# One hybrid layer on Trainium2: the turn at LN1 with four plain FF tiles, a scan with fewer vector steps, and early forms for the output projection

## The chip, the cores and the metric

One core of a Trainium2 chip runs the kernel. The time is device time in microseconds (us) of one execution; lower is better. Five engines run their own queues in order: TensorE (PE, matrix products; weight loads are shown as PEld), VectorE (DVE), ScalarE (ACT), GpSimd (POOL) and SyncE (SP), which issues most DMA transfers. [...]

## The reference

One layer with a sequence of 1024 positions, width 1024 and FF width 4096, all in float32:

```python
mods = (silu(c) @ ada_w + ada_b); sh1, sc1, g1, sh2, sc2, g2 = split(mods, 6)
h = x * (1 + sc1) + sh1
# Mamba-2 mixer: z, xBC, dt = h @ w_in; causal conv of 4 and silu on xBC;
# chunked state-space scan, 8 groups of 4 heads of 64, state 128; y += D * xs;
# y = rmsnorm_per_group(y * silu(z)) * norm_w;  y = y @ w_out
x = layer_norm(alpha * x + g1 * y, ln1_g, ln1_b)
h = x * (1 + sc2) + sh2
x = layer_norm(alpha * x + g2 * (square(relu(h @ w1)) @ w2), ln2_g, ln2_b)
```

## The kernel before

Every large product is made of three products of 128 x 128 by 128 x 512: each operand is split into a high part (fp32r, made by an ACT or DVE cast, L117) and a low part (the rest, one subtraction on DVE or POOL, L120), and high x high, low x high and high x low are added in PSUM. "Forms" below means such a pair. The order of instructions on each engine is set by a planner that takes, engine by engine, the earliest instruction in program order that it believes ready; `issue_after` adds that an instruction stands behind a named one on its engine. Tiles live in pools; a pool opened after another is closed takes over its memory, and each of its tiles waits for the last readers of what lay there.

The stages:

- Head and scan (up to some 739 us). 45 weight tiles of the input projection (`proj`, L137) are streamed; between them the planner places 64 steps of the chunked scan (`ssd_chunk`, L318: 8 groups x 8 chunks), 16 gates (`gate`, L382: 8 groups x 2 halves of the sequence) and 8 conditioning blocks (`mods_block`, L419), one after every fifth weight tile. A chunk transposes x and B into the PSUM bank px, makes X (times dt), cbm, bt and xd (X times wend) on DVE, and the state product pst (L372) needs bt and xd. A gate squares and sums into the bank pr, takes the reciprocal root by Ln, Exp and a Newton step, scales y and stores it to DRAM on SP's queue (L416). A block loads four times 512 KB into one buffer, multiplies and adds on DVE (L427, L429) and sums over partitions with PE into the bank pr. Blocks 0 to 3 give shift and scale of the second half (mod2), 4 to 7 the gates g1b and g2b.
- Output projection (739 to some 950 us). Four passes, (T, Dh) = (0,0), (0,1), (1,0), (1,1), over halves of the sequence (T) and of the columns (Dh), `out_pass` L545; each has 16 steps of 12 matmuls. A step loads a piece of w_out and, in the passes with Dh = 0, of y (`out_load`, L522), and splits both: w_out's high part on ACT and low part (owl) on POOL. The forms of y for T = 0 lie in the blocks B of the pool `per`, which takes the place of the projection's input forms hh and hl. The passes use the PSUM pairs psm (T, 0) and ps2 (T, 1).
- LN1 and the turn (around 950 to 1030 us). `ln1(T)` (L583) normalises four rows, transposes them (L601) and makes h2 and its forms in B. Two FF tiles (`up_plain`, f = 0, 1) run T = 0 in PE's spare time and T = 1 after `ln1(1)`, then two more (f = 2, 3) run both halves. Meanwhile DVE makes sums of the four blocks of h2 (L707 to L712), whose forms t1 to t4 the rest of the FF tiles need: from f = 4 on tiles go in pairs (`up_quad`, L732) with seven block products in place of eight, and each pair needs sums of its w1 blocks (L738 to L741) and forms s1 to s4, a1 and a22.
- Down projection (some 1290 us to the end), `down`, then LN2.

Names: `NS = 4` (L668) is the number of plain tiles; `mpa` holds the w1 forms of f = 0, 1 in rings of two; `hk` and `lt` hold h2 of T = 0 and T = 1; `tpool` the forms t; `wp` the raw and split weights of the input projection; `load1` and `forms1` (L643, L648) load and split a w1 tile; `lg`, `lbb` (L638) are LN1's rows for the residual.

Of the kernel before, what the change touches and what calls it, by code (L numbers as in the profile page):

```python
# [34 lines left out]
def trunk(ctx: ExitStack, tc: tile.TileContext, a: dict, out: bass.AP):  # L35
# [23 lines left out]
    adab = consta([P, 6, KT], "adab")  # L59
# [5 lines left out]
    vec.memset(ones, 1.0)  # L65
    ones_r = consta([P, P], "ones_r", F32R)
# [13 lines left out]
    csil = consta([P, KT], "csil")  # L80
# [38 lines left out]
    def low(src, hi, lo, eng):  # L119
        eng.tensor_tensor(lo, src, hi.bitcast(F32), op=ALU.subtract)  # L120
# [197 lines left out]
    def ssd_chunk(g, c):  # L318
# [21 lines left out]
        if not last:  # L340
# [3 lines left out]
            vec.tensor_tensor(xd, X, wend[:, c, hs].unsqueeze(2).broadcast_to([P, HPG, HD]), op=ALU.mult)  # L344
# [37 lines left out]
    def gate(g, T):  # L382
# [25 lines left out]
        vec.tensor_tensor(q, m, q, op=ALU.mult)  # L408
        vec.scalar_tensor_tensor(r, q, 3.0, r, op0=ALU.subtract, op1=ALU.mult)
        for j in range(2):  # L410
# [4 lines left out]
            else:  # L415
                sp.dma_start(y_dram[2 * g + j][:, ts], gt[:, j, :])  # L416


    def mods_block(b):  # L419
# [23 lines left out]
    vec.tensor_scalar(nwcol, nwcol, -0.5, None, op0=ALU.mult)  # L443
# [21 lines left out]
    for n, (kind, g, j) in enumerate(slots):  # L465
# [56 lines left out]
    def out_load(T, Dh, k):  # L522
# [5 lines left out]
        if Dh == 0 and not (T == 0 and k >= 14):  # L528
# [173 lines left out]
    for T in range(2):  # L702
        up_plain((2, 3), ws2, T)
# [243 lines left out]
```

## Time and profile before

| | us |
|---|---|
| median of 3 runs (1655.02 to 1657.81) | 1656.39 |
| the profiled execution, its own time | 1657.81 |
| its span | 1656.1 |
| PE busy | 1574.5 (95%) |
| DVE busy | 1017.6 (61%) |
| ACT busy | 758.5 (46%) |
| POOL busy | 564.3 (34%) |

The profiled execution is one of the three runs. Times in the trace count from the start of its span. Busy time is the union of an engine's instructions; a wait is the idle time of an engine in front of an instruction, with the instruction that ended it. Most of the matmuls overlap, so a single one lasts 0.39 to 0.40 us but they start 0.23 us apart.

### The profile page before, as it was taken

How to read it: one execution, taken by the hardware profiler on the slowest of the kernel's cores; microseconds unless marked ns; L12 is line 12 of the kernel's file. 1: busy time of each engine (PE TensorE's matmuls, PEld its weight loads, DVE VectorE, ACT ScalarE, POOL GpSimd, SP SyncE). 2: the span in 40 equal slices, each digit the busy share in tenths (PEclk: the TensorE clock that was granted, in tenths of full speed). 3: DMA queues.
4: the chain of work that ended last, by engine and by line, in shares of the span. 5: the costliest groups of instructions: out<-in, count | busy, mean ns of one | idle time of the engine just before them, and what ended most of it. 6: DMA issues, size and time to landing. Idle time of an engine off the chain costs nothing.

```text
span 1656.1 us, 20252 instructions
## 1 busy us (share of the span) xinstructions
PE 1574.5 (95%) x7600; PEld 1264.8 (76%) x7600; DVE 1017.6 (61%) x1480; ACT 758.5 (46%) x1159; POOL 564.3 (34%) x305
## 2 busy tenths in 40 slices
PE   7999898999999899988899978999999999999997
PEld 5887686878777787766688856888888888878886
DVE  8757969787776757757754384545554542287335
ACT  3546557675647466765443153333333322333230
POOL 3313424342424224244645352322332222244221
PEclk9999999999999999999999989999999999999998
DMA  8324423333233222115764122232223655446541
GB/s 323 129 80 147 133 84 115 103 97 107 92 113 96 83 77 77 45 58 178 243 207 160 57 95 83 90 114 102 102 102 132 217 192 166 146 140 207 183 131 51
DMA packets 77138, 209.37 MB, mean 126 GB/s; under 512 B 9585, under 2 KB 11121, under 8 KB 76145
## 3 DMA queue, kind: packets, MB, share of 16 engines
q1 hardware_dynamic: 76176, 205.96, 37.2%
q0 software_dynamic: 576, 2.10, 0.3%
q8 instruction: 60, 0.98, 0.2%
q14 instruction: 38, 0.30, 0.1%
q10 hardware_dynamic: 288, 0.03, 0.0%
HBM read 174.89 MB, written 33.16 MB: 126 GB/s over the span
## 4 chain that ended last, share of the span: by engine, by line
PE 69%; DVE 17%; DMA 6%; issue 4%; ACT 3%; POOL 1%; SPq 0%; DVEq 0%; POOLq 0%; ACTq 0%
PE mm L836 20%; PE mm L144 19%; PE mm L729 16%; PE mm L542 7%; DMA adr<-in_ada_r_dram 2%; DVE mac L429 2%; PE mm L684 2%; DVE macc L203 1%; PE pst L372 1%; DVE y L411 1%; DVE hn L378 1%; DVE dec L349 1%; PE py L359 1%; DMA yr<-y_dram 1%; DMA ada<-in_ada_a_dram 1%
## 5 line engine op out<-in xcount | busy, mean ns | idle before, releaser
L144 PE MATMUL mm<-hh,whi 128*128 128x512 f32 x720 | 288.5, 401 | 0.0
L144 PE MATMUL mm<-hl,whi 128*128 128x512 f32 x720 | 287.4, 399 | 0.0
L144 PE MATMUL mm<-hh,wlo 128*128 128x512 f32 x720 | 286.3, 398 | 0.0
L836 PE MATMUL mm<-w2h,uh 128*128 128x512 f32 x512 | 197.9, 389 | 1.2 <-DVE tm L866 1.2
L836 PE MATMUL mm<-w2l,uh 128*128 128x512 f32 x512 | 198.2, 389 | 0.0
L836 PE MATMUL mm<-w2h,ul 128*128 128x512 f32 x512 | 197.6, 389 | 0.0
L120 POOL TENSOR_TENSOR wlo<-wraw,whi 128x1024 fp32r<-128x1024 f32 x45 | 111.8, 2484 | 233.1 <-ACT whi L117 233.1
L144 PEld LDWEIGHTS mm<-hh,wlo 128*128 128x128 f32 x720 | 136.5, 190 | 29.2 <-issue 1.8
L144 PEld LDWEIGHTS mm<-hh,whi 128*128 128x128 f32 x720 | 136.5, 190 | 28.9 <-issue 1.6
L144 PEld LDWEIGHTS mm<-hl,whi 128*128 128x128 f32 x720 | 136.5, 190 | 28.7 <-issue 1.1
L353 POOL TENSOR_TENSOR ea<-ea,Ct 128x512 f32<-128x512 f32 x56 | 79.4, 1418 | 192.3 <-ACT ea L352 187.0
L120 POOL TENSOR_TENSOR w2l<-w2r,w2h 128x1024 fp32r<-128x1024 f32 x30 | 75.0, 2502 | 185.8 <-ACT w2h L117 185.8
L120 DVE TENSOR_TENSOR ul<-ur,uh 128x512 fp32r<-128x512 f32 x62 | 49.8, 812 | 129.1 <-ACT uh L117 129.1
L347 ACT ACTIVATE dec<-ar,acs 128x128 f32<-128x128 f32 x256 | 81.6, 390 | 82.3 <-PE py L359 79.0
L120 POOL TENSOR_TENSOR owl<-owr,owh 128x512 fp32r<-128x512 f32 x64 | 90.1, 1416 | 85.0 <-ACT owh L117 82.7
L836 PEld LDWEIGHTS mm<-w2h,uh 128*128 128x128 f32 x512 | 96.1, 188 | 21.7 <-DVE tm L866 1.6
L836 PEld LDWEIGHTS mm<-w2l,uh 128*128 128x128 f32 x512 | 96.2, 188 | 20.2
L836 PEld LDWEIGHTS mm<-w2h,ul 128*128 128x128 f32 x512 | 96.1, 188 | 19.7
L117 ACT CAST uh<-ur 128x512 fp32r<-128x512 f32 x62 | 38.4, 621 | 154.0 <-PE mm L836 123.1
L117 ACT CAST w2h<-w2r 128x1024 fp32r<-128x1024 f32 x62 | 64.8, 1048 | 22.4 <-DMA w2r<-in_w_dram 13.4
L429 DVE SCALAR_TENSOR_TENSOR mac<-adr,csil,mac 128x512 f32<-128x512 f32 x56 | 60.2, 1076 | 21.8 <-DMA adr<-in_ada_r_dram 21.4
L349 DVE TENSOR_TENSOR dec<-dec,cbm 128x512 f32<-128x512 f32 x64 | 61.0, 953 | 19.3 <-ACT dec L348 19.3
(356 smaller groups left out, 3487.7 us busy)
## 6 DMA issues: line engine op xcount, KB each, us to landing
w2r<-in_w_dram SPq DMA_DIRECT2D x62, 512.0 KB, 3.7
wraw<-in_w_in_dram SPq DMA_DIRECT2D x45, 512.0 KB, 4.2
w1r<-in_w_dram SPq DMA_DIRECT2D x34, 512.0 KB, 3.7
adr<-in_ada_r_dram SPq DMA_DIRECT2D x32, 512.0 KB, 3.6
ar<-a_dram SPq DMA_DIRECT2D x64, 256.0 KB, 3.3
owr<-in_w_out_dram SPq DMA_DIRECT2D x64, 256.0 KB, 3.3
ur<-u_dram SPq DMA_DIRECT2D x62, 256.0 KB, 2.8
u_dram<-row SPq DMA_DIRECT2D x28, 512.0 KB, 3.8
```

What stands on the lines that cost most here:

```text
L117: return (act.copy if eng is act else eng.tensor_copy)(hi, src)
L120: eng.tensor_tensor(lo, src, hi.bitcast(F32), op=ALU.subtract)
L144: pe.matmul(ps[:, hf, :], lhsT=w_[:, k, :], rhs=x_[:, k, ts], start=(k == 0 and i == 0), stop=(k == KT - 1 and i == 2))
L203: vec.scalar_tensor_tensor(av_, ada[:, k, :], csil[:, k:k + 1], av_, op0=ALU.mult, op1=ALU.add)
L347: act.activation(dec[:, h, :], ar[:, h, :], AF.Relu, scale=-1.0, bias=acs[:, c, g * HPG + h:g * HPG + h + 1])
L349: vec.tensor_tensor(dec, dec, cbm.unsqueeze(1).broadcast_to([P, HPG, C]), op=ALU.mult)
L353: pool.tensor_tensor(ea, ea, G["C"][:, ts].unsqueeze(1).broadcast_to([P, HPG, C]), op=ALU.mult)
L429: vec.scalar_tensor_tensor(acc, ad[:, i, :], csil[:, k:k + 1], acc, op0=ALU.mult, op1=ALU.add)
L542: pe.matmul(po[t // 2][:, t % 2, :], lhsT=l_[:, t * P:t * P + P], rhs=r_, start=(k == 0 and i == 0), stop=(k == 15 and i == 2))
L684: pe.matmul(ups[f][:, T, :], lhsT=w_[:, k, :], rhs=x_[:, k % 4, :], start=(k == 0 and i == 0), stop=(k == KT - 1 and i == 2))
L729: pe.matmul(dst, lhsT=w_[:, k, :], rhs=x_[:, k, :], start=(first and k == 0 and i == 0), stop=(k == 3 and i == 2), skip_group_check=not first)
L836: pe.matmul(po[t][:, Dh, :], lhsT=l_[:, t * P:(t + 1) * P], rhs=r_[:, Dh * 512:Dh * 512 + 512], start=(f == 0 and i == 0), stop=(f == NF - ...
```

## The change

- Scan: six conditioning blocks, in the order 4, 5, 6, 7, 0, 1, one after every seventh weight tile; blocks 2 and 3 are made by a new function `mods_ln1` behind the second output pass, with their loads in the eight tiles of `hk` and their sum in a psm tile. wend is multiplied by dt once, and xd is made from px and that in place of X. In the gate Ln reads pr with scale and bias; m is gone, and the Newton step reads pr. The y of groups 6 and 7 is stored from POOL's queue.
- Output projection: steps 0 and 1 of the first pass load into `wraw`, and their forms are made in the buffers `whi`, `wlo` and in a tile of group 6's x, ahead of the projection's end. The second pass loads and splits y for these two steps again.
- Turn: the w1 loads stand behind w_out's. All four plain tiles run T = 0 together, behind step 13 of the fourth pass, and then T = 1 in pairs; tiles 2 and 3 have forms of their own (`pf`). The sums of h2 are held behind the last low part of h2; low parts for T = 1 go to DVE. The first pair's sums lie in tiles with the tags of lg and lbb, its forms in those of h2 (`lt`, `hk`), its a1 low part on DVE. t1 takes the place of `pf`. The second pair takes its second product ahead of s3's. lg and lbb are loaded and scaled in the down projection.

```diff
-            vec.tensor_tensor(xd, X, wend[:, c, hs]..., op=ALU.mult)
+            vec.tensor_tensor(xd, px[:, 0:2 * P]..., wend[:, c, hs]..., op=ALU.mult)
...
-        m = ssp.tile([P, 512], F32, name="m", tag="s1")
-        vec.tensor_scalar(m, pr, 1.0 / 256.0, EPS, op0=ALU.mult, op1=ALU.add)
-        act.activation(r, m, AF.Ln)
+        act.activation(r, pr, AF.Ln, scale=1.0 / 256.0, bias=eps_c)
...
-        vec.tensor_tensor(q, m, q, op=ALU.mult)
-        vec.scalar_tensor_tensor(r, q, 3.0, r, op0=ALU.subtract, op1=ALU.mult)
+        vec.scalar_tensor_tensor(q, pr, 256.0 * EPS, q, op0=ALU.add, op1=ALU.mult)
+        vec.scalar_tensor_tensor(r, q, 768.0, r, op0=ALU.subtract, op1=ALU.mult)
...
-                sp.dma_start(y_dram[2 * g + j][:, ts], gt[:, j, :])
+                (pool if g >= NG - 2 else sp).dma_start(y_dram[2 * g + j][:, ts], gt[:, j, :])
...
-        if n % 5 == 0 and n // 5 < 8:
-            mods_block(n // 5)
+        if n % 7 == 0 and n // 7 < 6:
+            mods_block((4, 5, 6, 7, 0, 1)[n // 7])
...
+    yx = gp.tile([P, 2, S], F32R, name="yx", tag="xs")
+    early = []
+    for k in range(2):
+        raw = wp.tile([P, 2, 512], F32, name="wraw", tag="wraw", bufs=4)
+        sp.dma_start(raw[:, 0, :], a["w_out"][k][:, 0:512])
+        sp.dma_start(raw[:, 1, :], y_dram[k][:, 0:512])
+        w = [wp.tile([P, 512], F32R, name="w" + q, tag="w" + q) for q in ("hi", "lo")]
+        y = (yx[:, k, 0:512], yx[:, k, 512:S])
+        split(raw[:, 0, :], *w, act, pool)
+        split(raw[:, 1, :], *y, act, vec)
+        early.append((w, y))
     phR.close()
...
+        if k == 13:
+            queue["k13"] = mm_.ins
...
+    def mods_ln1(b):
+        ad = []
+        for k in range(KT):
+            t_ = hk.tile([P, 512], F32, name="adm", tag=f"h2{k % 2}{k // 2}")
+            sp.dma_start(t_, a["ada_r"][b, k // 2][:, k % 2, :])
+            if k == 0:
+                vec.tensor_scalar(t_, t_, csil[:, 0:1], None, op0=ALU.mult)
+            else:
+                vec.scalar_tensor_tensor(t_, t_, csil[:, k:k + 1], ad[-1], op0=ALU.mult, op1=ALU.add)
+            ad.append(t_)
+        pm = psm.tile([P, 2, 512], F32, name="mm", tag="mm")
+        for i in range(4):
+            pe.matmul(pm[:, 0, i:i + 1], lhsT=ad[-1][:, i * P:(i + 1) * P], rhs=one1, start=True, stop=True)
+        mod2_add(b, pm[:, 0, 0:4])
...
-                low(h2, bh[:, kk, :], bl[:, kk, :], vec if kh == 0 else pool)
+                queue["h2l"] = low(h2, bh[:, kk, :], bl[:, kk, :], vec if kh == 0 or T == 1 else pool).ins
...
     out_pass(0, 1, po)
+    for b in (2, 3):
+        mods_ln1(b)
...
-        sp.dma_start(w1r, a["w1"][f])
+        load_behind(w1r, a["w1"][f], "w")
...
-    up_plain((0, 1), ws1, 0)
-    ln1(1, sts)
-    up_plain((0, 1), ws1, 1)
-    ws2 = [forms1(load1(f)) for f in range(2, NS)]
-    for T in range(2):
-        up_plain((2, 3), ws2, T)
+    for f in range(2, NS):
+        ws1.append(forms1(load1(f), [pf.tile([P, KT, P], F32R, name=f"p{q}{f}", tag=f"p{q}{f}") for q in "hl"]))
+    with tc.issue_after(queue["k13"]):
+        up_plain(0)
+    ln1(1, sts)
+    up_plain(1)
+    up_evict(0)
...
+    with tc.issue_after(queue["h2l"]):
+        for kk in range(4):
+            b11, b12, b22 = h2f[0, 0, kk], h2f[0, 1, kk], h2f[1, 1, kk]
+            t1_ = vec.tensor_tensor(b11, b12, b11, op=ALU.subtract)
+            vec.tensor_tensor(b12, b22, b12, op=ALU.subtract)
+    t_split("t3", lambda kk: h2f[0, 1, kk], vec)
+    with tc.issue_after(t1_.ins):
+        for kk in range(4):
+            b11, b21, b22 = h2f[0, 0, kk], h2f[1, 0, kk], h2f[1, 1, kk]
+            vec.tensor_tensor(b22, b22, b11, op=ALU.subtract)
+            vec.tensor_tensor(b21, b21, b22, op=ALU.subtract)
+    t_split("t2", lambda kk: h2f[1, 1, kk], vec)
...
+    r0_, a22_ = quad_sums(NS // 2, s_)
+    a1_ = forms1(r0_, eng=vec)
+    quad_splits(s_, F_)
+    up_evict(1)
+    pfx.close()
+    tl = tst.enter_context(tc.tile_pool(name="tl", bufs=1, side="right", reuse_waits="tile"))
+    TF["t1"] = [tl.tile([P, 4, 512], F32R, name="t1" + q, tag="t1" + q) for q in "hl"]
     TF["t4"] = h2_block("b12")
+    t_split("t1", lambda kk: h2f[0, 0, kk], pool)
+    t_split("t4", lambda kk: h2f[1, 0, kk], pool)
...
+            if T == 0 and f == 2:
+                load_behind(lg, a["ln_rows"][0:1, :].partition_broadcast(P).squeeze(1), "w2")
+                load_behind(lbb, a["ln_rows"][1:2, :].partition_broadcast(P).squeeze(1), "w2")
+                vec.tensor_scalar(lg, lg, ALPHA, None, op0=ALU.mult)
+                vec.tensor_scalar(lbb, lbb, ALPHA, None, op0=ALU.mult)
```

## Rows read from the trace of the kernel before

**Rows 1.** Stages: start:end, length, busy us (instructions) by engine, clock, DMA share, GB/s

```profile
115.00:739.00 624.00, 597.98 (x3355) 476.68 (x3354) 453.00 (x775) 387.43 (x615) 210.83 (x109) 0.99 0.30 97
739.00:820.00 81.00, 67.92 (x302) 50.63 (x301) 60.32 (x74) 42.78 (x73) 43.17 (x27) 0.96 0.59 195
820.00:950.00 130.00, 130.00 (x584) 106.61 (x584) 52.96 (x78) 42.68 (x70) 63.03 (x47) 1.00 0.46 148
950.00:1060.00 110.00, 92.26 (x366) 69.86 (x365) 71.04 (x77) 46.31 (x70) 43.15 (x22) 0.91 0.23 79
1060.00:1290.00 230.00, 230.00 (x987) 185.21 (x987) 119.86 (x128) 76.34 (x129) 69.08 (x35) 1.00 0.34 118
1290.00:1656.00 366.00, 354.06 (x1559) 292.27 (x1558) 176.07 (x207) 108.58 (x147) 101.21 (x42) 0.99 0.47 157
```

**Rows 2.** The same view of two short stretches; the order is PE, PEld, DVE, ACT, POOL

```profile
743.00:746.40 3.40, 3.22 (x7) 2.28 (x8) 2.98 (x3) 3.26 (x7) 3.40 (x3) 0.50 0.23 63
...
982.00:992.20 10.20, 7.40 (x16) 5.13 (x17) 9.36 (x5) 6.75 (x8) 8.81 (x4) 0.50 0.45 129
```

**Rows 3.** PE's waits, 950 to 1030: in total us, times, longest us

```profile
PE mm L684 <- ACT w1h L117: 5.1, 2, 4.1
PE mm L684 <- DVE b12l L120: 4.0, 2, 3.2
```

**Rows 4.** PE's time line in the turn: start, us, instruction [idle before]

```profile
956.59 0.65 PE L601 MATMUL mm<-ident,row 128*128 128x128 f32 x4 [1.57 <-ACT row L593]
...
959.79 0.77 PE L684 MATMUL mm<-b12h,w1h 128*128 128x512 f32 x1
```

**Rows 5.** DVE's groups, 957 to 992: count, busy us, mean ns, idle before

```profile
L712 DVE TENSOR_TENSOR h<-h,h 128x512 f32<-128x512 f32 x4 | 6.0, 1492 | 0.0
...
L708 DVE TENSOR_TENSOR h<-h,h 128x512 f32<-128x512 f32 x4 | 2.7, 678 | 0.0
```

**Rows 6.** POOL's groups, 957 to 1031, the same view

```profile
L120 POOL TENSOR_TENSOR t2l<-h,t2h 128x512 fp32r<-128x512 f32 x4 | 6.4, 1599 | 2.0 <-ACT t2h L117 1.9
```

**Rows 7.** PE's waits in the scan, 115 to 739

```profile
PE pst L372 <- DVE xd L344: 9.3, 8, 3.4
...
PE pst L372 <- DVE hn L379: 5.1, 3, 3.5
```

**Rows 8.** DVE's groups in the scan, 115 to 739

```profile
L429 DVE SCALAR_TENSOR_TENSOR mac<-adr,csil,mac 128x512 f32<-128x512 f32 x56 | 60.2, 1076 | 21.8 <-DMA adr<-in_ada_r_dram 21.4
...
L344 DVE TENSOR_TENSOR xd<-X,wend 128x256 f32<-128x256 f32 x56 | 33.6, 599 | 0.0
L336 DVE TENSOR_TENSOR X<-px,dt 128x256 f32<-128x256 f32 x63 | 26.2, 415 | 12.7 <-PE py L359 7.1 <-PE px L334 5.3
...
L402 DVE TENSOR_SCALAR m<-pr 128x512 f32<-128x512 f32 x12 | 8.2, 687 | 29.6 <-PE pr L400 29.6
```

**Rows 9.** Waits of DVE for the loads of the conditioning blocks: us, times

```profile
  DMA adr<-in_ada_r_dram: 29.3, 15
```

**Rows 10.** PE's waits, 739 to 820

```profile
PE mm L542 <- POOL owl L120: 6.0, 6, 2.1
PE mm L542 <- ACT y L117: 3.7, 1, 3.7
```

**Rows 11.** POOL's time line: the second of two w1 low parts there

```profile
795.93 2.84 POOL L120 TENSOR_TENSOR w1l<-w1r,w1h 128x1024 fp32r<-128x1024 f32 x1
```

**Rows 12.** DVE's time line: a conditioning block's first and last instruction, two evictions' starts

```profile
451.61 0.48 DVE L427 TENSOR_SCALAR mac<-adr,csil 128x512 f32<-128x512 f32 x1
...
479.52 0.73 DVE L429 SCALAR_TENSOR_TENSOR mac<-adr,csil,mac 128x512 f32<-128x512 f32 x1
...
805.77 1.28 DVE L621 TENSOR_TENSOR tm<-mm,g1b 128x512 f32<-128x512 f32 x2
...
849.97 1.29 DVE L621 TENSOR_TENSOR tm<-mm,g1b 128x512 f32<-128x512 f32 x2 [2.51 <-PE mm L542]
```

**Rows 13.** DMA issues from POOL's queue: ns min/median/max, first and last start

```profile
L688 POOL DMA_DIRECT2D u_dram<-row x4: 531/596/736, 1281.0 to 1303.8; - x4
```

More of the change, by code (lines that the diff above doesn't have):

```diff
@@ L305, in trunk @@
             act.activation(dst.rearrange("p a b -> p (a b)"), pa, fn)
+    vec.tensor_tensor(wend, wend, dt, op=ALU.mult)
     acsf = acs.rearrange("p a b -> p (a b)")
@@ L527, in out_load @@
         yr = None
-        if Dh == 0 and not (T == 0 and k >= 14):
+        if (Dh == 0 and not (T == 0 and k >= 14)) or (T == 0 and k < 2):
             yr = ob_pool.tile([P, 512], F32, name="yr", tag="yr")
@@ L547, in out_pass @@
         for k in range(16):
-            ws.append(out_load(T, Dh, k))
+            first = T == 0 and Dh == 0 and k < 2
+            ws.append(early[k][0] if first else out_load(T, Dh, k))
             ks = [k] if k < 16 - KL else range(16 - KL, 16) if k == 15 else []
@@ L551, in out_pass @@
                 for k_ in ks:
-                    out_mms(po, k_, t, ws[k_], yt[k_])
+                    out_mms(po, k_, t, ws[k_], early[k][1] if first else yt[k_])
             if Dh == 0 and T == 1 and k % 4 == 0:
@@ L673, in trunk, with up_plain @@
     ups = {}
-    def up_plain(fs, ws, T):
-        for f in fs:
-            if T == 0:
-                pl_, tg = (psm, "mm") if f % 4 < 2 else (ps2, "mm2")
-                ups[f] = pl_.tile([P, 2, 512], F32, name=tg, tag=tg)
-        for k in (0, 4, 1, 5, 2, 6, 3, 7):
+    def up_plain(T):
+        pl_, tg = ((psm, "mm"), (ps2, "mm2"))[T]
+        for i in range(NS // 2):
+            ups[T, i] = pl_.tile([P, 2, 512], F32, name=tg, tag=tg)
+        for k, f in [(k, f) for f0 in range(0, NS, NS if T == 0 else 2) for k in (0, 4, 1, 5, 2, 6, 3, 7)
+                     for f in range(f0, NS if T == 0 else f0 + 2)]:
@@ L681, in up_plain @@
             bh, bl = B[k // 4, T]
[L682 to L685 removed]
+            w = ws1[f]
+            for i, (w_, x_) in enumerate(((w[0], bh), (w[1], bh), (w[0], bl))):
+                pe.matmul(ups[T, f // 2][:, f % 2, :], lhsT=w_[:, k, :], rhs=x_[:, k % 4, :],
+                          start=(k == 0 and i == 0), stop=(k == KT - 1 and i == 2))
@@ L713, in trunk, with up_evict @@
-    up_evict(0)
-    up_evict(1)
-    for kk in range(4):
-        split(h2f[1, 0, kk], TF["t4"][0][:, kk, :], TF["t4"][1][:, kk, :], act, vec if kk % 2 else pool)
-    for f in range(2, NS):
-        up_evict(f)
-    lt1.close()
-    hkx.close()
-    mp = up_.enter_context(tc.tile_pool(name="mp", bufs=1, reuse_waits="tile"))
+    us = {}
+    def up_evict(T):
+        for f in range(NS):
+            if T == 0:
+                us[f] = rowp.tile([P, S], F32, name="row", tag="row")
+            act.activation(us[f][:, T * 512:T * 512 + 512], ups[T, f // 2][:, f % 2, :], AF.Relu)
+        if T == 1:
+            for f in range(NS):
+                act.activation(us[f], us[f], AF.Square)
+                u_store(f, us[f])
@@ L775, in up_quad @@
         u_store(f0, u0)
-    for p in range(NS // 2, NF // 2):
+    up_quad(NS // 2)
+    lt1.close()
+    hkx.close()
+    mp = up_.enter_context(tc.tile_pool(name="mp", bufs=1, reuse_waits="tile"))
+    for p in range(NS // 2 + 1, NF // 2):
         up_quad(p)
```

131 lines of the change are left out of this document (69 added, 62 removed).

## The prediction

> **What bounds it.** I read the table by stages first, then, stage by stage, the waits of TensorE (PE), then the time lines of the engines that end those waits. From 1060 to 1290 us PE has no idle time and issues 987 matmuls in 230 us, 0.233 us each [rows 1]: that is the pace at which this kernel costs nothing to improve but matmuls, and the change removes no matmul. So the gain can only come out of idle time and of stretches at the lower clock, and these lie in three places [rows 1]. The scan (115 to 739): 624.0 - 598.0 = 26.0 us idle, and a mean granted clock of 0.99, worth some 6 us more. The step into the output projection (739 to 820): 13.1 us idle, clock 0.96. The turn at LN1 (950 to 1060): 17.7 us idle at a clock of 0.91. Between them, 820 to 950, PE is busy throughout. For the turn I make the account by pace: 366 records, of which 32 are the short transposes of `ln1(1)`; 334 x 0.233 = 77.8, and eight groups of four transposes at no more than 0.65 [rows 4] = 5.2; 110.0 - 83.0 = 27.0 us lost. [...]
>
> **The sum** is made against the profiled execution: span 1656.1, its own time 1657.81, which is the slowest of the three runs shown and 1.4 above their median.
>
> **A, the LN1 turn.** The waits there are for w1h casts, for b12l and for the first rows [rows 3]. Of 96 plain T=1 and late T=0 matmuls those of tiles 2 and 3 come only when tiles 0 and 1 have given back their w1 buffers; and the low parts of h2 queue on VectorE (DVE) between sums that belong to the next step. The change gives tiles 2 and 3 buffers of their own, runs T=0 of all four in a row (96 x 0.233 = 22.4 us) while rows are evicted, normalised and transposed, and holds the sums back behind the last low part. The turn itself needs about 10 us: the last pass ends near 950, the first transpose starts at 956.59, the first T=1 matmul at 959.79 [rows 4]. 22.4 us cover it, so these waits go. What is left, piece by piece:
> (a) if the 96 stand ahead of the transposes in PE's queue, PE waits once from the first transpose to the first forms: 959.79 - 956.59 = 3.2, less two groups of transposes, 1.3 [rows 4]: 2 us.
> (b) the next bound is DVE. From the last low part of h2, PE still has 12 + 48 plain matmuls and two products of 12 before it needs the s2 forms: 84 x 0.233 = 19.6 us. In that time DVE does 16 sums, 8 low parts of t3 and t2, 4 sums of the quad and 2 of its low parts, 30 instructions of 512 columns, and one low part of 1024 (1.4, about two of them). An instruction of this form took 0.678 on average in one group and 1.492 in another of the same stretch [rows 5]; the second group ran beside GpSimd (POOL). With d us each, the shortfall is 30d + 1.4 - 19.6. The change takes POOL out of this stretch (the low parts of h2, t3, t2 and of the quad all go to DVE), so I take d = 0.68: 2.2 us.
> (c) t1, t4 and a22 come on POOL after the last plain matmul, because t1 lies where the forms of tiles 2 and 3 were: 8 x 1.599 [rows 6] + 1.7 = 14.5 us against five products, 60 x 0.233 = 14.0: 0.5 to 3, I take 2.
> (d) one or two stretches of 3.4 us at the lower clock after such waits: 3.4.
> Together 9.6 left of 27.0: A = 17. Ends: 5 (d = 1.1) and 23.
> The same number of matmuls is only moved: some 27 of the T=0 matmuls that ran inside the fourth pass now run behind it, where they are the cover.
>
> **B, the scan.** All its longest PE waits are for DVE: xd 9.3, hn 5.1 and others [rows 7]. DVE gives up: two of eight `mods_block`s, a quarter of 60.2 us of mac [rows 8] and of 29.3 us in which DVE stood for their 512 KB load [rows 9], 22 us; xd read from PSUM, as X is, 56 x (0.599 - 0.415) = 10.3 us [rows 8]; m, 16 x 0.687 = 11.0 us [rows 8]. 43 of its 453 busy and some 37 waiting us. If PE's idle time shrank only in that proportion, it would be 2 to 3 us; if every wait for xd and a quarter of the rest went, 13, and the clock with it. I take B = 8, ends 2 and 16. Two small costs: px and the bank of pr are held longer (xd and q read them), for one DVE step and for three ScalarE (ACT) steps; PE's next transpose or sum waits if it comes in that time. [...] The rows differ, 0.415 from PSUM and 0.599 from SBUF [rows 8], and the sum goes by them.
>
> **C, into the output projection.** PE waits 3.7 us for the first y cast, and 6.0 in six waits for owl, POOL's low part of w_out [rows 10]. Steps 0 and 1 now have their forms in the buffers of the projection in front, and the first no longer waits: 3.7, and with it the slow stretch from 743.0 to 746.4, where 7 matmuls took 3.4 us in place of 15 [rows 2]: 1.6. The first w1 low parts, two of 2.5 to 2.8 us on POOL, stand between those of w_out there [rows 11]; their loads now go behind the last w_out load of the third pass: 2. Against it, six y stores move from SyncE's (SP) queue to POOL's, 0.6 each [rows 13], ahead of owl, and steps 0 and 1 of the second pass load and split y again: -1. C = 6. Ends 1, if the gates' own chain sets the end, and 10.
>
> **D, the moved mods.** Blocks 2 and 3 now run after the first pass's eviction starts, 805.77, in the second pass: 16 loads of 256 KB on SP among the w_out loads, 16 DVE instructions, 8 matmuls. They hold psm, which the third pass needs when the second ends; the second's eviction starts at 849.97 [rows 12]. DVE has room (53 of 130 us busy, [rows 1]). In the scan one block took from 451.61 to 480.3 [rows 12], 28.6 us, with one buffer; two such would end at 863, 13 us late. With eight buffers the loads of a block come together, two blocks of 8 x 1.08 [rows 8] fit into 44 us. I take 3 for w_out loads held up behind the burst; ends 0 and 13.
>
> **At nothing:** the LN1 scale rows, loaded and scaled in the down projection (two instructions on a DVE busy 176 of 366 us there, [rows 1]; if they landed late, the first x1 row would be late, not PE), the wend product, the later a1 and quad order.
>
> Sum: 17 + 8 + 6 - 3 = 28; 1657.8 - 28 = 1629.8, and 1628.4 on the scale of the median; I say 1628.
>
> **Rivals.** (1) DVE bounds the turn in part: POOL still runs beside it and d is 1.1, the middle of the two groups [rows 5]. (b) becomes 33 + 1.4 - 19.6 = 14.8, 22 us stay lost, A = 5: 1657.8 - 5 - 8 - 6 + 3 = 1642. For it: the low parts of f2 and f3 on POOL may slip into the turn. Against it: POOL has nothing else there.
> (2) The scan keeps its idle time because the waits move with the order (B = 0), and the mods end late (D = -13): 1657.8 - 17 - 6 + 13 = 1648. For it: mac and hn stand in one queue, whatever xd does.
> (3) The change doesn't do what it says: forms made in buffers of the stage in front wait for that stage's last reader, so early forms are not early, and a gain of a few us is given back by D: 1655 to 1659.
> (4) Slower, by one mechanism: in the turn's second half DVE's instructions run at the lengths seen beside POOL throughout, since t1, t4 and the quad's forms all wait for buffers of the stage in front and pile up in one heap. At d = 1.8, (b) is 35.8, 43 us are lost in place of 27, A = -16, and 1657.8 + 16 - 8 - 6 + 3 = 1663. It decides where 30d - 18.2 + 7.4 = 27 + 11, from d = 1.63. For it: the group at 1.492 [rows 5]. Against it: that group ran beside POOL's b22l, t2l and w1l, which the change moves or ends.
>
> **Chances.** Forecast 0.55 (its own range 1612 to 1641), rival 1 0.18, rival 2 0.12, more than forecast (A = 23, B = 16, C = 10, D = 0: 1609) 0.02, rival 3 0.05, rival 4 0.08. A measurement of this kernel can tell some 0.2%, 3 us, from no change: faster 0.87, same 0.05, slower 0.08. The range 1610 to 1649 takes in rivals 1 and 2 and leaves out 0.15.
>
> **What would show it.** A right: between the last w_out matmul and the second quad no PE wait over 3 us, 334 matmuls and 32 transposes in some 93 us; DVE's sums there near 0.68. B right: fewer than 20 us idle in the scan, waits for xd under 5. C right: no wait of 3 us at the first step. D right: the third pass follows the second without a wait. The forecast is wrong if the sums in the turn take over 1.1 us, or if the scan's idle time stays at 26 us.

## The result, and the profile after

The changed kernel takes 1637.06 us (median of four runs, 1632.64 to 1641.63) against 1656.76 for the kernel before on the same chip; the ratio is 0.9882, with a 95% interval of 0.9851 to 0.9914. That is faster by 1.2%, as forecast, and inside the range, but 9 us slower than the 1628 forecast. The profiled execution of each kernel is its slowest: 1657.81 (span 1656.1) before and 1641.63 (span 1639.9) after, 16.2 us apart. Both traces were cut at the same instructions, and so were those of the experiments: the first and last matmul of the weight tiles (scan), the start of the evictions of the first three passes of the output projection, the last w_out matmul, the first matmul of the first pair (turn) and the first of the down projection (pairs). Lengths in us, from the time lines; "step" runs from the last weight tile's matmul to the first eviction, so it holds the first pass. Each kernel was profiled in one of its runs, and the lengths are that run's, while the times are medians. The ratios are to the kernel before as it ran beside each of them, with medians of 1654.63 to 1656.76 us; compare the ratios rather than the times.

| kernel | time | ratio to before (95%) | scan | step | pass 2 | pass 3 | pass 4 | turn | pairs |
|---|---|---|---|---|---|---|---|---|---|
| before | 1656.76 | | 674.0 | 67.2 | 44.2 | 49.2 | 51.0 | 63.6 | 273.2 |
| after | 1637.06 | 0.9882 (0.9851-0.9914) | 660.4 | 62.6 | 53.1 | 54.3 | 51.3 | 45.6 | 277.7 |
| e1 | 1635.51 | 0.9874 (0.9855-0.9893) | 662.9 | 63.2 | 44.5 | 53.4 | 50.8 | 45.6 | 273.6 |
| e2 | 1633.09 | 0.9855 (0.9838-0.9871) | 660.0 | 63.1 | 50.9 | 57.1 | 49.9 | 45.6 | 272.2 |
| e3 | 1629.46 | 0.9838 (0.9820-0.9855) | 658.8 | 62.7 | 50.1 | 51.0 | 50.0 | 45.6 | 274.3 |
| e4 | 1633.08 | 0.9857 (0.9836-0.9878) | 660.5 | 61.1 | 49.6 | 55.0 | 49.9 | 45.6 | 278.7 |
| e5 | 1646.73 | 0.9941 (0.9927-0.9955) | 663.1 | 68.5 | 43.8 | 49.2 | 51.0 | 63.2 | 273.5 |
| e6 | 1636.39 | 0.9874 (0.9858-0.9890) | 657.0 | 64.7 | 48.6 | 53.4 | 51.1 | 45.6 | 276.6 |
| e7 | 1629.30 | 0.9839 (0.9824-0.9854) | 664.2 | 65.8 | 44.8 | 50.9 | 50.0 | 45.6 | 272.8 |
| e8 | 1628.98 | 0.9831 (0.9817-0.9845) | 664.6 | 64.2 | 43.9 | 50.7 | 49.8 | 45.6 | 275.8 |
| e9 | 1629.18 | 0.9843 (0.9825-0.9861) | 659.0 | 62.2 | 53.2 | 50.6 | 50.1 | 45.6 | 273.1 |
| e10 | 1634.80 | 0.9879 (0.9861-0.9896) | 660.4 | 62.3 | 53.3 | 50.1 | 50.1 | 45.6 | 279.3 |
| e11 | 1632.13 | 0.9867 (0.9852-0.9882) | 659.5 | 61.6 | 51.7 | 53.3 | 51.4 | 45.6 | 274.0 |
| e12 | 1628.74 | 0.9845 (0.9830-0.9859) | 658.0 | 68.1 | 50.6 | 49.2 | 50.2 | 45.6 | 272.7 |

The head (before the scan) takes 64.0 to 66.8 and the down projection 369.0 to 369.3 in all of them. The stages after, from the table by stages (columns as in [rows 1], with TensorE's granted clock as a share of full speed; the first stage is cut at 115 us, as there):

```profile
115.00:726.31 611.31, 595.07 (x3343) 475.31 (x3342) 424.68 (x745) 412.39 (x636) 211.00 (x110) 0.99 0.29 93
726.31:788.92 62.61, 53.90 (x246) 40.44 (x245) 40.76 (x56) 37.65 (x62) 31.38 (x25) 0.89 0.50 155
788.92:842.03 53.11, 49.21 (x209) 39.99 (x208) 32.54 (x43) 14.43 (x24) 22.25 (x16) 0.94 0.73 248
842.03:896.37 54.34, 50.14 (x227) 40.87 (x226) 24.73 (x42) 25.09 (x40) 32.22 (x22) 0.94 0.59 198
947.68:993.27 45.59, 43.85 (x203) 34.94 (x201) 30.28 (x58) 24.79 (x40) 7.40 (x1) 1.00 0.21 81
993.27:1270.96 277.69, 270.19 (x1142) 216.18 (x1141) 139.23 (x147) 94.81 (x160) 92.50 (x49) 0.99 0.32 109
```

The scan is 13.6 us shorter, the step 4.6, the turn 18.0. Then look at the third and fourth line: passes 2 and 3, in which TensorE had next to no idle time before, have lost clock (0.94) and 8.1 us of idle time, and are 8.9 and 5.1 us longer. Of the 18.2 us that the scan and the step won, some 4 are left at the fourth pass. Together with the pairs (+4.5), pass 4 (+0.4) and the head (+1.3, less 0.3 in the down projection) this is the sum: 13.6 + 4.6 + 18.0 - 8.9 - 5.1 - 4.5 - 0.4 - 1.0 = 16.3, but for rounding.

TensorE's waits in passes 2 and 3 (789 to 900), and ScalarE's longest in pass 2:

```profile
PE mm L559 <- POOL owl L122: 4.8, 2, 4.2
PE mm L606 <- DVE adm L602: 2.9, 1, 2.9
...
ACT owh L119 <- DMA owr<-in_w_out_dram: 15.9, 3, 6.6
```

L606 is the one-column matmul of the moved conditioning blocks; owl is w_out's low part on GpSimd. Behind the longer waits come stretches at a lower clock, in which matmuls start 0.43 us apart in place of 0.23, so that about half the length of such a row of matmuls is lost: here, in the table by stages, those among the step's waits (which are shown under e6), behind L606 and behind owl, with a clock of 0.50 or 0.51.

```profile
736.70:750.40 13.70, 8.35 (x18) 4.88 (x20) 9.80 (x12) 6.29 (x11) 5.94 (x7) 0.50 0.41 142
808.40:815.20 6.80, 6.48 (x19) 5.51 (x20) 6.62 (x11) 1.24 (x2) 1.27 (x1) 0.50 0.89 291
890.30:897.20 6.90, 4.65 (x11) 3.69 (x12) 2.60 (x4) 0.00 (x0) 3.43 (x3) 0.51 0.25 76
```

The queue behind the wait for L606, SyncE's time line (the moved blocks' loads are adm, L598):

```profile
789.14 0.38 SPq L543 DMA_DIRECT2D owr<-in_w_out_dram  x1
789.63 6.02 SPq L598 DMA_DIRECT2D adm<-in_ada_r_dram  x7
796.00 0.33 SPq L543 DMA_DIRECT2D owr<-in_w_out_dram  x1
...
801.22 7.02 SPq L598 DMA_DIRECT2D adm<-in_ada_r_dram  x6
```

Twice, six or seven of these loads, 6 to 7 us in all, stand between two w_out loads: in that time a pass at full pace uses up more than two steps of 12 matmuls (12 x 0.23 = 2.8 us each). And GpSimd's time line at the end of pass 3:

```profile
881.92 2.41 POOL L122 TENSOR_TENSOR w1l<-w1r,w1h 128x1024 fp32r<-128x1024 f32 x1 [2.85 <-ACT w1h L119]
884.29 1.74 POOL L122 TENSOR_TENSOR owl<-owr,owh 128x512 fp32r<-128x512 f32 x1
886.00 2.39 POOL L122 TENSOR_TENSOR w1l<-w1r,w1h 128x1024 fp32r<-128x1024 f32 x1
888.35 2.48 POOL L122 TENSOR_TENSOR b21l<-h,b21h 128x512 fp32r<-128x512 f32 x2
890.79 2.94 POOL L122 TENSOR_TENSOR owl<-owr,owh 128x512 fp32r<-128x512 f32 x2
```

These are the w1 low parts of [rows 11], 90 us later. They were not taken off GpSimd's path to w_out, only moved along it.

### The profile page after: what moved, and what is told of

It is laid out like the page before. It is cut to its first block, busy times and chain, and to the rows that moved or that the text cites. A ratio compares the mean times of both kernels' runs of the same rounds, so it can differ in the third digit from the quotient of the medians.

```text
span 1639.9 us, 20287 instructions
## 1 busy us (share of the span) xinstructions
PE 1573.5 (96%) x7600; PEld 1268.6 (77%) x7600; DVE 978.0 (60%) x1473; ACT 784.4 (48%) x1183; POOL 555.5 (34%) x306
## 4 chain that ended last, share of the span: by engine, by line
PE 76%; DVE 11%; DMA 6%; ACT 3%; issue 3%; POOL 1%; SPq 0%; DVEq 0%; POOLq 0%; ACTq 0%
PE mm L146 22%; PE mm L919 20%; PE mm L798 16%; PE mm L559 6%; PE mm L714 3%; DMA adr<-in_ada_r_dram 3%; DVE mac L437 2%; PE py L364 2%; PE pst L377 1%; PE py L369 1%; DMA yr<-y_dram 1%; PE mm L230 1%; DVE xs L159 1%; DVE macc L205 1%; DMA ada<-in_ada_a_dram 1%
## 5 line engine op out<-in xcount | busy, mean ns | idle before, releaser
L122 POOL TENSOR_TENSOR wlo<-wraw,whi 128x1024 fp32r<-128x1024 f32 (+1 forms) x47 | 113.6, 2418 | 224.3 <-ACT whi L119 218.2
L122 POOL TENSOR_TENSOR owl<-owr,owh 128x512 fp32r<-128x512 f32 x62 | 85.5, 1387 | 87.9 <-ACT owh L119 87.8
L159 DVE SCALAR_TENSOR_TENSOR xs<-mm,convw,xs 128x1023 f32<-128x1023 f32 (+2 forms) x45 | 57.6, 1279 | 35.4 <-ACT xs L153 34.7
L119 ACT CAST owh<-owr 128x512 fp32r<-128x512 f32 x62 | 38.1, 619 | 81.0 <-PE mm L559 45.2
```

What stands on the lines that cost most here:

```text
L119: return (act.copy if eng is act else eng.tensor_copy)(hi, src)
L122: return eng.tensor_tensor(lo, src, hi.bitcast(F32), op=ALU.subtract)
L159: vec.scalar_tensor_tensor(dst[:, j:S], src[:, 0:S - j], convw[:, ct, 3 - j:4 - j], dst[:, j:S], op0=ALU.mult, op1=ALU.add)
```

## Experiments on passes 2 and 3

The theory after the traces: two separate stalls, one from the moved blocks in pass 2 and one from the w1 low parts in pass 3, give back what was won.

**e1: all eight blocks in the scan again.**

```diff
-        if n % 7 == 0 and n // 7 < 6:
-            mods_block((4, 5, 6, 7, 0, 1)[n // 7])
+        if n % 5 == 0 and n // 5 < 8:
+            mods_block(n // 5)
...
-    for b in (2, 3):
-        mods_ln1(b)
```

> All eight conditioning blocks stand in the scan again, one after every fifth weight tile; the rest is the changed kernel. Theory (the burst of blocks 2 and 3 costs the second pass some 8 us, and the scan's gain comes mainly from xd and the gate): the second pass of the output projection falls from 53.2 us back to about 45, the input projection ends some 4 us later than at 726.3, and the time is 1633 us against 1637. Rival (the scan's gain comes from the two blocks that left it): the input projection ends 9 us later or more, at 735 or behind it, and the time is 1638 to 1645.

Measured: pass 2 44.5, scan 662.9, 1635.5 us. The stage went as the theory said, and the scan paid 2.5 us for two more blocks. The row of pass 2, as above (clock 1.00, 0.6 us idle):

```profile
791.15:835.67 44.52, 43.90 (x193) 35.79 (x192) 16.02 (x21) 14.40 (x24) 22.03 (x16) 1.00 0.60 204
```

Over all kernels of the table with the moved blocks pass 2 is 48.6 to 53.3 (mean 51.2), over the others 43.8 to 44.8 (44.2): 7.0 us for the blocks. The scan takes 657.0 to 660.5 with six blocks (mean 659.3) and 662.9 to 664.6 with eight and the new steps (e1, e7, e8; 663.9): 4.6 back. So the scan returns most of the price, and the time of e1 can't be told from that of the changed kernel.

**e2: the one-column matmuls behind step 13 of pass 2.**

```diff
+        with tc.issue_after(queue["k13"]):
             for i in range(4):
                 pe.matmul(pm[:, 0, i:i + 1], lhsT=ad[-1]..., rhs=one1, ...)
```

> The eight one-column matmuls of the moved conditioning blocks stand behind step 13 of the second pass; their loads and vector steps stay. Theory (TensorE stands at these matmuls for the vector chain, 2.9 us and then 3.4 us at half clock): the second pass falls from 53.2 us to 48, with the two small waits for w_out's loads left; the time falls by 0 to 5 us, as far as the third pass's wait for GpSimd does not take it. Rival (the wait for w_out's loads behind the burst is what costs): the second pass stays above 51 us.

Measured: pass 2 50.9, just under the rival's 51 and far from the theory's 48, and pass 3 57.1 (the eight matmuls now fall behind the boundary); the two together take 108.0 against 107.4. The wait for adm fell to 0.4, and this stood in its place:

```profile
811.65 0.73 PE L559 MATMUL mm<-owh,b21h 128*128 128x512 f32 x2 [1.55 <-ACT owh L119]
813.48 0.79 PE L559 MATMUL mm<-owl,b21h 128*128 128x512 f32 x1 [1.10 <-POOL owl L122]
```

So the theory's account of this stall was wrong and the rival's right: with the matmuls out of the way TensorE waits for w_out's loads behind the burst, and its waits in pass 2 add up to 3.8 us in place of 3.9. The vector chain and the loads are both late behind the same burst; taking away the wait for one shows the other.

**e3: the low parts of the first two w1 tiles on VectorE.**

```diff
-    ws1 = [forms1(load1(f)) for f in range(2)]
+    ws1 = [forms1(load1(f), eng=vec) for f in range(2)]
```

> The low parts of the first two w1 tiles are made by VectorE in place of GpSimd. Theory (in the third pass they and b21l stand ahead of w_out's low parts on GpSimd, a wait of 4.2 us and then a stretch at half clock): the third pass falls from 54.8 us to 48 or 49, the time by some 6 us to 1631. Rival (b21l alone holds the queue, or w_out's loads are late): the third pass stays above 52 us. Second rival: the vector steps now delay the eviction or the rows of LN1, and the gain is lost at the turn.

Measured: pass 3 51.0, between the theory's 49 and the rival's 52, its longest wait 1.4 in place of 4.2, and 1629.46 us: 0.0044 of the time of before (7 us) below the changed kernel, though the intervals touch. The kernels with these two low parts on VectorE have a pass 3 of 50.1 to 51.0 (e3, e7 to e10); those with them on GpSimd 53.3 to 54.3 (after, e1, e6, e11); e2 and e4, whose boundary is moved, are left out of both. The one wait that is left in pass 3, 1.4 us, is for the owl that stands behind the second pair of b21l on GpSimd.

**e4: the edits of e2 and e3 together.**

> Both edits together: the one-column matmuls behind step 13 of the second pass, and the low parts of the first two w1 tiles on VectorE. Theory (two separate stalls, each of 5 to 7 us): second pass 48 us, third pass 48 to 49 us, time 1626 us, faster than the changed kernel by 9 to 12 us. Rival (the passes are held by the output projection's own loads, so that what one stall gives back the next one takes): 1632 to 1637.

Measured: 1633.08 us, passes 2 and 3 49.6 and 55.0, together 104.6 against 101.2 in e3. The rival was right: e2's edit on top of e3's adds nothing. (The time alone would not show it, for in its profiled run this kernel also lost some 4 us in the pairs, as told under e10.)

**e12: the loads of these two w1 tiles not bound behind w_out's last.**

```diff
-    ws1 = [forms1(load1(f)) for f in range(2)]
+    ws1 = [forms1(load1(f, True)) for f in range(2)]
...
+        if now:
+            sp.dma_start(w1r, a["w1"][f])
+        else:
             load_behind(w1r, a["w1"][f], "w")
```

> The changed kernel with the loads of the first two w1 tiles no longer bound behind w_out's last load of the third pass. Theory (the bound moved their low parts on GpSimd from the step into the output projection to the end of the third pass, where they cost the wait of 4.2 us): third pass 49 to 51 us in place of 54.3, and from the last matmul of the input projection to the first eviction 64 to 66 us in place of 62.6; the time 2 to 4 us below the changed kernel's. Rival (GpSimd is free enough in the first pass): the third pass falls and the step stays at 62.6; the time falls by 5 or more.

Measured: pass 3 49.23 without a wait, as the theory said, and the step 68.1, longer even than its 64 to 66. The two stages, then GpSimd's time line in the step:

```profile
722.28:790.41 68.13, 56.16 (x248) 41.78 (x246) 42.85 (x57) 39.42 (x64) 37.38 (x27) 0.87 0.48 159
840.98:890.21 49.23, 49.23 (x232) 40.58 (x231) 25.16 (x42) 23.20 (x38) 27.27 (x20) 1.00 0.57 197
...
775.29 2.37 POOL L122 TENSOR_TENSOR w1l<-w1r,w1h 128x1024 fp32r<-128x1024 f32 x1 [2.12 <-ACT w1h L119]
777.62 1.71 POOL L122 TENSOR_TENSOR owl<-owr,owh 128x512 fp32r<-128x512 f32 x1
779.30 2.38 POOL L122 TENSOR_TENSOR w1l<-w1r,w1h 128x1024 fp32r<-128x1024 f32 x1
781.65 3.42 POOL L122 TENSOR_TENSOR owl<-owr,owh 128x512 fp32r<-128x512 f32 x2
```

The same two instructions cost some 5 us in either place: +5.5 here, -5.1 there. The time nevertheless came out at 1628.74, by the ratios 6 us below the changed kernel's, more than the theory's 2 to 4; by the stages the difference lies in head, scan, pass 2 and pairs, which this edit does not touch. The section on the turn and the pairs explains part of that (the pairs, 5.0); the rest stays open.

**e7: the edits of e1 and e3 together.**

> The changed kernel with all eight conditioning blocks in the scan and the low parts of the first two w1 tiles on VectorE. Theory (both stalls in the second and third pass have their causes removed, where moving the one-column matmuls had only handed the stall to w_out's loads): scan 663 us, second pass 44.5, third 49 to 51, time 1624 to 1627. Rival (the third pass is held by its own loads): third pass 53 or more, time 1630 or more.

Measured: scan 664.2, passes 2 and 3 44.8 and 50.9 as expected, but the step 65.8, and 1629.30 us, the same as e3 and not the 1624 to 1627 of the theory. With pass 2 mended the scan and the step are 8.5 us longer than in e3. So where the two blocks stand is worth nothing that these runs can tell.

## Experiments on the scan and the first steps

**e5: the kernel before with the scan's vector edits alone.**

```diff
+    vec.tensor_tensor(wend, wend, dt, op=ALU.mult)
...
-            vec.tensor_tensor(xd, X, wend[:, c, hs]..., op=ALU.mult)
+            vec.tensor_tensor(xd, px[:, 0:2 * P]..., wend[:, c, hs]..., op=ALU.mult)
...
-        vec.tensor_scalar(m, pr, 1.0 / 256.0, EPS, op0=ALU.mult, op1=ALU.add)
-        act.activation(r, m, AF.Ln)
+        act.activation(r, pr, AF.Ln, scale=1.0 / 256.0, bias=eps_c)
...
```

> The kernel before with only the scan's vector edits: xd from px, dt put into wend once, the gate without m. All eight blocks stay. Theory (the shorter vector steps of chunk and gate carry the scan's gain, since putting the two blocks back cost it only 2.5 us): the stretch from the first weight tile's matmul to the last falls from 674.0 us to 663 to 665, the time from 1656 to 1645 to 1647. Rival (the gain came from the order of the blocks and from what is laid behind the scan): the stretch stays at 670 us or more, the time at 1653 or more.

Measured: scan 663.1, 1646.73 us, ratio 0.9941 (0.9927 to 0.9955), all as the theory said: 10.9 of the scan's 13.6 us come from these edits. How they divide between the chunk's and the gate's was not tried. TensorE's waits in its scan, which answer to [rows 7], and the two groups of [rows 8]:

```profile
PE pst L374 <- DVE xd L345: 6.2, 6, 3.1
PE pmr L434 <- DVE mac L430: 3.2, 2, 1.8
PE py L361 <- DVE y L370: 3.2, 3, 2.3
...
L337 DVE TENSOR_TENSOR X<-px,dt 128x256 f32<-128x256 f32 x63 | 26.1, 414 | 8.6 <-PE px L335 8.0
L345 DVE TENSOR_TENSOR xd<-px,wend 128x256 f32<-128x256 f32 x56 | 22.9, 409 | 0.0
```

xd fell from 599 to 409 ns, and the waits for bt (5.7 before) and hn (5.1) are gone from the list, although neither was edited: they share a queue with xd and m. The wait that bears xd's name is still there, 6.2 of 9.3.

**e6: the changed kernel without the early forms of steps 0 and 1.**

```diff
-            ws.append(early[k][0] if first else out_load(T, Dh, k))
+            ws.append(out_load(T, Dh, k))
...
```

> The changed kernel without the forms made ahead for the output projection's first two steps. Theory (the first wait of 3.7 us and its slow stretch come back): from the last matmul of the input projection to the first eviction 66 to 67 us in place of 62.6, the time some 4 us above the changed kernel's. Rival (the last gates' sums and the load of the next y set the end of this stretch either way): 62 to 64 us, no difference in the time.

Measured: 1636.39 us, the step 64.7, between the theory's 66 and the rival's 64. The first wait came back, at 6.2 us (3.7 in [rows 10]); it is gone in the changed kernel, whose waits in the step are shown below it:

```profile
PE mm L550 <- ACT y L119: 6.2, 1, 6.2
PE mm L550 <- POOL owl L122: 3.3, 1, 3.3
...
PE mm L559 <- ACT b11h L119: 3.6, 1, 3.6
PE pr L404 <- DVE sh L119: 2.7, 2, 1.6
```

b11h there is y's high part for the third step. TensorE walks through the two early steps and then waits for the third, whose y comes into the buffers of the projection; and the sums of the last gates, which stand in its queue there, wait for their own chain. Early forms for two steps shorten the step by 2.1 us: it takes 61.1 to 63.1 in the seven kernels that have them with six blocks in the scan and w1's loads as changed. The time shows no difference, as the rival said.

## Experiments on the turn and the pairs

**e11: four low parts of the turn (b22l) on GpSimd again.**

```diff
-                queue["h2l"] = low(..., vec if kh == 0 or T == 1 else pool).ins
+                low_ = low(..., vec if kh == 0 else pool)
+                if kh == 0:
+                    queue["h2l"] = low_.ins
```

> The changed kernel with four low parts of h2 of T = 1 (b22l) on GpSimd, as before the change. Theory (VectorE's instructions run at 0.69 us in the turn because GpSimd is out of it; beside GpSimd they take 1 to 1.5): single low parts and sums of VectorE rise to 1.0 or more while GpSimd works, and the turn, from the last matmul of the output projection to the first of the first pair, takes 47 to 51 us in place of 45.6, although VectorE has four instructions less. Rival (the length of the turn is set by TensorE's own work by now): 45.6 us.

Measured: the turn takes 45.59 us, to the hundredth what it takes in the changed kernel, so the rival is right. VectorE's sums did stretch: the first row is the changed kernel (955 to 1000), the others this one: the same group of sums, and GpSimd's part.

```profile
L752 DVE TENSOR_TENSOR h<-h,h 128x512 f32<-128x512 f32 x4 | 2.5, 684 | 0.0
...
L754 DVE TENSOR_TENSOR h<-h,h 128x512 f32<-128x512 f32 x4 | 4.7, 1235 | 0.0
...
L122 POOL TENSOR_TENSOR b22l<-h,b22h 128x512 fp32r<-128x512 f32 x4 | 5.9, 1484 | 31.2 <-ACT b22h L119 31.2
```

Four sums at 1.235 in place of 0.684 us cost TensorE nothing: it has its own work through the whole turn. The run does not show what a late VectorE would cost, for the four low parts that left its queue (2.8 us) weigh about what the stretched ones added, and s2's low part was ready some 11 us ahead of its use in both kernels.

**e8 and e9: the wait at the second pair's s3.** In the changed kernel, and in every one with its turn but e8, TensorE waits 1.7 us for s3h and 1.0 for s3l there. e8 (on e7) casts s3h on VectorE and issues the first two pairs' u stores from GpSimd; e9 (on e3) gives s3's forms another place and lays s2's over the first pair's s4 forms.

```diff
-            split(src, F[nm][0], F[nm][1], act, eng)
+            split(src, F[nm][0], F[nm][1], e3 if nm == "s3" else act, eng)
...
-        (pool if f >= NF - 4 else sp).dma_start(u_dram[f], u)
+        (pool if f >= NF - 4 or NS <= f < NS + 4 else sp).dma_start(u_dram[f], u)
```

The first hunk is e8's alone, with e3 = vec for the second pair; the second is in e8 and in e10. And e9:

```diff
+    F_["s2"][1], F_["s4"][1] = F_["s4"][1], F_["s2"][1]
...
-            F.update({nm: form(nm) for nm in ("s3", "s2")})
+            F.update({nm: form(nm) for nm in ("s2", "s3")})
```

> As the run with the blocks in the scan and the low parts on VectorE, and besides the second pair's s3 high part cast by VectorE and the u stores of the first two pairs issued from GpSimd. Theory (in the pairs TensorE waits because s3's cast stands on ScalarE behind the first pair's last eviction, and w1's loads behind its u stores on SyncE): the pairs' stretch, from the first pair's first matmul to the down projection's first, falls from 272 to 278 us to 269 to 270, time 1621 to 1624. Rival (the buffers that the second pair takes over come free only then): the stretch stays above 272.

> The run with the low parts of the first two w1 tiles on VectorE, and in it other places for the second pair's s3 forms: they lie where the first pair's s2 low part and nothing of the first pair lay, and s2's forms take the place of the first pair's s4 forms, which TensorE reads last. Theory (the second pair's s3 cast waits for the first pair's last product because it overwrites that product's operand): the waits for s3h and s3l at the second pair (1.7 and 1.0 us) go, the stretch from the first pair's first matmul to the down projection's first falls from 274.3 us to 269 to 272, the time from 1629 to 1625 to 1628. Rival (the casts stand behind ScalarE's last eviction of the first pair, whatever the place): no change, 272 us or more.

Measured: the pairs take 275.8 and 273.1 us against 272.8 (e7) and 274.3 (e3); the times are those of e7 and e3. Both theories failed (in e8 the waits became 0.5 for s3h and 2.4 for s3l), and the rows say why. e8's cast on VectorE, then ScalarE's line in e9:

```profile
1012.05 0.43 DVE L119 CAST s3h<-s 128x512 fp32r<-128x512 f32 x1 [2.38 <-PE mm L796]
...
1015.17 0.60 ACT L851 ACTIVATE row<-mm 128x512 f32<-128x512 f32 x1 [2.23 <-PE mm L799]
1015.66 0.61 ACT L119 CAST a22h<-w1r 128x512 fp32r<-128x512 f32 x1
1016.17 0.62 ACT L119 CAST s3h<-s 128x512 fp32r<-128x512 f32 x1
```

Off ScalarE the cast still waits for the first pair's last product, whose operand it overwrites; in a free place it still stands behind ScalarE's eviction of that product. Each cause hides the other. Both edits together were not tried.

**e10: e9 with the u stores of the first two pairs on GpSimd** (the second hunk above).

> As the run with the new places of the second pair's forms, and the u stores of the first two pairs issued from GpSimd. Theory (w1's loads for the third pair stand behind u stores on SyncE, and so its sums and its s3 forms are late): the wait at the third pair's s3 goes too, the stretch of the pairs falls to 268 to 270 us, the time to 1623 to 1627. Rival (those loads wait for their three buffers, not for the queue): no further change from the run with the new places alone.

Measured: 1634.80 us, 5.6 slower than e9, pairs 279.3. Neither the theory nor the rival foresaw a loss. It goes with one instruction, s3l of the third pair. VectorE and GpSimd in the changed kernel, in e9 and in e10:

```profile
1034.29 2.85 DVE L122 TENSOR_TENSOR s3l<-s,s3h 128x512 fp32r<-128x512 f32 x1
1034.25 2.34 POOL L122 TENSOR_TENSOR w1l<-w1r,w1h 128x1024 fp32r<-128x1024 f32 x1 [0.44 <-ACT w1h L119]
...
1027.70 0.69 DVE L122 TENSOR_TENSOR s3l<-s,s3h 128x512 fp32r<-128x512 f32 x1
1028.11 2.53 POOL L122 TENSOR_TENSOR w1l<-w1r,w1h 128x1024 fp32r<-128x1024 f32 x1 [1.61 <-ACT w1h L119]
...
1027.86 2.83 DVE L122 TENSOR_TENSOR s3l<-s,s3h 128x512 fp32r<-128x512 f32 x1
1027.28 2.87 POOL L122 TENSOR_TENSOR w1l<-w1r,w1h 128x1024 fp32r<-128x1024 f32 x1 [0.60 <-ACT w1h L119]
```

Where GpSimd's w1l starts first, s3l takes 2.8 us in place of 0.69 and TensorE waits 3.7 to 3.95 us for it, with a slow stretch behind it. That is so in after, e4 and e10, whose pairs take 277.7 to 279.3; in the nine others s3l starts first, by 0.15 to 1.3 us, and their pairs take 272.2 to 276.6. In the profiled execution of the changed kernel GpSimd was first by 0.04 us. So some 4 of its 1641.63 us go with a race that its code does not settle. No edit here changed this order alone; the link rests on the twelve profiles, and on the same behaviour in the scan of the kernel before (next section). It may also lie behind the spread of the four runs, which the profile of one can't show.

## Why the prediction came out, and where its terms were off

The terms against the profiled pair: A 18.0 in the turn, less 0.4 in pass 4 and 4.5 in the pairs, 13.1 (forecast 17); B 13.6 (8); C 4.6 - 5.1 = -0.5 (6); D -8.9 (-3). The sum is 17.3 less 1.0 of head and tail, against 28.

**A** was right in its mechanism, and its price held in the turn. d was 0.68 to 0.69 in VectorE's groups, as taken; no wait in the turn passes 0.53 us, and the largest before the second pair is 0.94. Rivals 1 and 4 fall with this. The whole loss of [rows 3] is gone (14.4 us of idle time to 1.7), and the turn's clock is 1.00, without a stretch at 0.50 like the second of [rows 2]. By the prediction's own test, 366 matmuls and transposes behind the last w_out matmul take 95.9 us (forecast 93; 110.3 before). One piece was wrong, to the good: (b) has TensorE wait 2.2 us for the s2 forms, and the trace shows VectorE 11 us ahead.

```profile
991.47 0.69 DVE L122 TENSOR_TENSOR s2l<-sq,s2h 128x512 fp32r<-128x512 f32 x1
...
1002.87 0.40 PE L798 MATMUL mm<-t2h,s2h 128*128 128x512 f32 x1
```

The last low part of h2 ends at 975.36, so TensorE comes to the s2 forms 27.5 us later, and not the 19.6 of 84 matmuls. (Nor did some 27 of the T=0 matmuls move behind the fourth pass: 23 still run inside it.) What the sum missed is behind the turn: the first pair's forms lie where the second pair's come next, and the second and third pair now wait; before, the pairs cost 273.2. Over the nine kernels with the changed kernel's code in this stage the mean is 274.7, so the change costs some 1.6 there on average, and 4.5 is one outcome of the race.

**B** came out 5.6 above the sum, inside its ends. The step that failed is the price by named waits, "if every wait for xd and a quarter of the rest went": the instructions that were shortened relieve whatever queues behind them (bt, hn), and 10.9 us came from the vector edits alone. The idle time fell to 16.2, under the 20 named. The waits for xd stayed at 7.6, over the 5 named: that test was badly chosen. Rival 2 falls: the scan did not keep its idle time.

The 10.3 us for xd came out in amount (33.6 us of busy time to 23.1), for another reason than the prediction's: the 0.599 of [rows 8] is not the price of a source in SBUF. In the kernel before, 40 of the 56 xd have no GpSimd instruction beside them and take 405 to 418 ns, 411 on average; from PSUM, after the change, the mean is 413. Twelve started while a GpSimd instruction was running, took 0.63 to 2.58 us, and each ended some 0.28 us after that instruction. The longest, GpSimd's line and VectorE's:

```profile
187.20 2.84 POOL L120 TENSOR_TENSOR wlo<-wraw,whi 128x1024 fp32r<-128x1024 f32 x1
187.73 2.58 DVE L344 TENSOR_TENSOR xd<-X,wend 128x256 f32<-128x256 f32 x1
```

After the change 22 of the 56 have GpSimd beside them, and none takes more than 0.42 us. So reading px bought no cheaper read, with 413 ns against 411; it took xd out of GpSimd's way.

**C** failed in the 2 us for the w1 low parts. The prediction booked their leaving the step as a gain and asked of GpSimd's queue only there. They are two instructions of 2.4 us that stand ahead of owl wherever they go, and in pass 3, with b21l in the same queue, they cost 5.1; e12 shows the exchange in both directions. And the first wait, 3.7 + 1.6 in the sum, moved to the third step: 2.1 was left of it (e6). The test given for C (no wait of 3 us at the first step) was met, and the 3.6 us stood at the third. Rival 3 was true for this part: the step behind the early forms waits for the stage in front.

**D** was mis-sized. The 3 us "for w_out loads held up behind the burst" measured 8.9 in the profiled run and 7.0 on average; the end of 13 held it. Its reason was named, but not priced: two bursts of 6 to 7 us on SyncE, behind which a w_out load still needs 5.2 us to land (the median in that stretch; 3.7 in the first 26 us of pass 2 before the change), against the 3 x 12 x 0.23 = 8.3 us that w_out's three buffers cover. The test given for it ("the third pass follows the second without a wait") was met, and missed the loss inside the second.

C and D failed in the same way: of moved work the sum asked whether its busy time fits, and not who stands behind it in the new place. That the time still lies inside the forecast's own range (to 1641) is in part luck: without the 5.6 us that B gave beyond its price it would have been some 1643.

## What to carry to other kernels

Work moved off one queue position is paid for where it lands: list the instructions that will stand behind it there, on every queue that it uses, and price the longest of them against the buffers that cover it. When a stall has two causes that end together, removing one shows nothing; look at what ended second before you edit. Before you take a price from the mean of a group, look at its single instructions: a few may have been held by something else. Where two engines stop each other, the instruction that TensorE waits for should not start just behind the other's longest one (here s3l: it took 2.85 us when GpSimd's w1l had started first, and 0.69 when it started ahead of w1l).

## What the runs showed of the hardware

**VectorE and GpSimd held each other up, and the first one won.** The twelve xd above (0.63 to 2.58 us in place of 0.41) show one direction, and so does s3l, with 2.85 us in place of 0.69. The other: beside the longest unbroken row of VectorE instructions of the changed kernel's turn GpSimd's w1l took 9.14 us, where it takes 2.4 in pass 3. The row began at 974.67, ahead of w1l, and ended at 992.76, and w1l 2.25 us later.

```profile
985.87 9.14 POOL L122 TENSOR_TENSOR w1l<-w1r,w1h 128x1024 fp32r<-128x1024 f32 x1 [46.02 <-ACT w1h L119]
```

What makes one of them wait for the other no trace shows; on who waits for whom the traces agree: in the third pair's s3l of the twelve kernels with this turn, down to a lead of 0.04 us; in the four xd of the kernel before that started ahead of a GpSimd instruction and took 0.41 us like the free ones; and in X and the new xd, which read px in PSUM and were never held (X takes 405 to 425 ns in the 18 of 63 cases with GpSimd beside it, and 407 to 427 in the others).

**The burst of loads stood near 400 GB/s, and each load took longer.** In the 40 equal slices of 786 to 812 us, where w_out, rows and the blocks' loads run together, the rate stands between 378 and 416 GB/s in 19 slices on end, and a 256 KB load of either kind takes 5.2 us to land; the last row is w_out's in the kernel before, 803 to 829:

```profile
GB/s 321 88 79 202 221 394 315 321 397 347 378 416 416 388 403 407 407 403 410 407 407 410 407 403 403 407 403 403 410 347 246 268 101 236 132 154 303 243 186 344
...
owr<-in_w_out_dram SPq DMA_DIRECT2D x8, 256.0 KB, 5.2
...
owr<-in_w_out_dram SPq DMA_DIRECT2D x9, 256.0 KB, 3.7
```

Over the whole pass it moved 236 GB/s before the change and 248 after. Loads that fit by the mean rate had no room for 4 MB at once.
